# Attention in a hybrid decoder layer: values' products emitted three units behind the scores instead of two

## The chip, the cores and the metric

The kernel runs on one core of one Trainium2 chip. Its engines are TensorE (PE in the profile, its weight loads PEld), VectorE (DVE), ScalarE (ACT), GpSimd (POOL) and SyncE (SP), which issues most of the loads. The metric is device time of one execution in microseconds (us). The kernel before took 2129.9 us (median of 3 runs, 2129.59 to 2132.04).

## The reference

One inference step through two layers, for a prompt of 2048 tokens and for 8 sample sequences of 8 new tokens each with 1024 cached tokens. Layer 0 has a pooling mixer and differential attention side by side, layer 1 is gated linear attention. The change is in the prompt's attention of layer 0: 4 heads, each with two 64-wide query/key maps and a 128-wide value. For a block of 128 queries and all keys up to the diagonal:

```python
sc = jnp.einsum('bqhcd,bkhcd->bhcqk', qi, k)          # two maps c
sc = jnp.where((qpos[:, None] >= kpos[None, :])[None, None, None], sc, -jnp.inf)
p = jax.nn.softmax(sc, axis=-1)
a = p[:, :, 0] - lam_full * p[:, :, 1]
return jnp.einsum('bhqk,bkhe->bqhe', a, v)
```

The result is normalised per head (RMSNorm), multiplied by a gate and goes, together with the pooling mixer's output, through an output projection and a LayerNorm.

## The kernel before

**Units.** The prompt's attention is cut into 64 units (t, h): 128 queries of block t (0 to 15) of head h against 128 * (t + 1) keys. `units` (L1109) makes them in order: head 0 with all t; then head 1 with all t; then heads 2 and 3 in turn for each t. A unit has two parts.

`scores(t, h)` (L992): for each of the two maps c, the scores are matmuls into PSUM (L1016, L1017, the mask of the diagonal L1019), in pieces that hold two PSUM banks; there are two such places. DVE takes the negated row maximum (L1021 or L1024, joined by L1034), ACT writes the exponentials to SBUF and sums them (L1036). At the end DVE joins the two maps in the first one's buffer, `e0 + c2 * e1` (L1045), after the small steps L1039, L1043 and L1044.

`pv(t, h)` (L1051): for up to 4 blocks of 128 keys at a time, TensorE transposes the joined probabilities into one PSUM bank (L1068), ACT copies them out (`aT`, L1073), and TensorE multiplies them with the values into another bank (L1061). Then the result is copied (`oq`, L1088), and squares, RMS scale and gate follow on DVE and POOL (L1090 to L1099). For heads 0 and 1 the pair of blocks is stored (L1104); for heads 2 and 3 it stays in SBUF.

**Distance.** `self.pend` holds units whose scores are made and whose `pv` isn't. While the scores of a unit are emitted, the oldest of the list is emitted between them, piece by piece. `pend` is not emptied between the heads; `drain` (L1132) does it after the last unit.

**Buffers of the exponentials.** Four buffers (`ae0` to `ae3`, L919) and a fifth (`ae4`, L929) are in the list `self.e`. A unit takes two from its head (L1004) and writes map 0 to the first, map 1 to the second. The second comes back to the list's end after L1045 (L1047), the first when `pv` has emitted its last transposition (L1078). The two places come back in the order in which these are emitted. A new tenant's first write waits for the last reader of the old one.

**Values.** There is one place for the values of even heads and one for those of odd heads (L950), so head 3's first values (`vt`) are loaded when head 1's last products are done.

**What runs beside it.** `weave` (L869) emits other work between the units, in proportion to estimated costs: with head 0 the pooling mixer's part of the output projection (`out_pool`), with head 1 the whole attention of the samples (`Sample`, which loads the cached keys and values `sk` and `sv`), and with heads 2 and 3 the attention's part of the output projection and the LayerNorm (`out_attention`, L1196; its tiles are `otp`, `op`, `oyp`). A pair of tiles of the latter is emitted only when `A.done` (set at L1106) says that head 3's `pv` of a later block has been emitted (L1255). After that come layer 1's projections.

**Order.** The program text gives the order of emission. A planner then fixes each engine's own order before the program runs: in a simulated time of its own it takes, of the instructions that are ready, the one emitted first; the instructions of `scores` count as emitted 300 places earlier (`high_priority(300)`, L1011 and L1032). On the chip each engine goes through its fixed order and waits where an input or a buffer isn't ready.

Of the kernel before, what the change touches and what calls it, by code (L numbers as in the profile page):

```python
# [394 lines left out]
def layers(tc, d):  # L395
# [6 lines left out]
    with ExitStack() as left:  # L402
# [12 lines left out]
        for m, j in project_even(tc, d, P, P2, W, slot, psf):  # L415

            if (m, j) == (7, 3):

                keep = odd.enter_context(tc.tile_pool(name="keep", bufs=2, side="right", **rw))
                A = Attention(tc, d, right, psf, keep)  # L420
                A.load_k(0, 0)
                A.minus_lambda()
                A.load_q(0, 0)
            elif (m, j) == (5, 3):
                A.room_weights()
                units = A.units([0], [1])
            elif m == 3 and j % 2:
                next(units)
# [8 lines left out]
        A.load_v(0, 0)  # L437
        A.room_results()
        weave(units, fill, HEAD_COST, 17 * 8 * 640)
    with tc.tile_pool(name="as", bufs=2, **rw) as sp:  # L440
        weave(A.units([1], [2, 3]), Sample(tc, d, sp, A).gen(), HEAD_COST, 8 * 10300.0)
# [442 lines left out]
class Attention:  # L884
# [224 lines left out]
    def units(self, heads, after):  # L1109


        for t in range(16):
            for h in heads:
                if t % 4 == 2 and t < 14:
                    self.load_kv(h, t // 4 + 1)
                if t % 2 == 1 and t < 15:
                    self.load_q(h, t // 2 + 1)
                if t == 14 and h == heads[0]:
                    for n in after:
                        self.load_kv(n, 0)  # L1120
                        self.load_q(n, 0)
                old = self.pend.pop(0) if len(self.pend) == 2 else None
                for c in self.scores(t, h):
                    yield c
                    c = next(old, None) if old else None
                    if c is not None:
                        yield c
                if old:
                    yield from old
                self.pend.append(self.pv(t, h, *self.cur))  # L1130
# [1312 lines left out]
```

## Time and profile before

| | us |
|---|---|
| median of 3 runs | 2129.9 |
| the profiled execution's own time | 2135.73 |
| its span, first to last instruction | 2133.9 |
| TensorE busy | 2005.8 |
| VectorE busy | 1486.8 |
| ScalarE busy | 1005.2 |
| GpSimd busy | 878.9 |

The profile comes from one execution. A row of groups or of the timeline names the line of the kernel, the engine, the operation, what it writes and reads, its shape and how often it ran; then its busy time, the mean of one in ns, and the idle time of the engine just before it, with the instruction that ended that idle time (the releaser). The attention of head 0 runs from about 520 us, that of head 1 from about 710 us, that of heads 2 and 3 from about 880 to 1220 us.

### The profile page before, as it was taken

The page shows a single profiled execution, that of the slowest core. Times are in us where ns is not written, and L with a number is a line of the kernel's source. Part 1 is how long each engine was busy: PE and PEld are TensorE (multiplying, and loading weights), DVE is VectorE, ACT ScalarE, POOL GpSimd, SP SyncE. Part 2 cuts the span into 40 slices and gives each one's busy share as a digit, 9 for nine tenths or more (in the row PEclk, how much of TensorE's full clock was granted, in tenths as well). Part 3 has the DMA queues.
Part 4 walks back from the last instruction along what each step waited for, and adds up shares of the span by engine and source line. Part 5 has one row for each costly group of instructions (what it writes and reads, how often), then busy time and mean ns, then how long its engine had stood idle before and what let it go on. Part 6 is the DMA issues. An engine that isn't in the chain of part 4 may idle for free. (4 is left out here: it accounts for less than half of the span.)

```text
span 2133.9 us, 31445 instructions
## 1 busy us (share of the span) xinstructions
PE 2005.8 (94%) x10769; PEld 1641.6 (77%) x10769; DVE 1486.8 (70%) x2762; ACT 1005.2 (47%) x1910; POOL 878.9 (41%) x1163
## 2 busy tenths in 40 slices
PE   8999998999999999888898899999999997999998
PEld 7878786877788777677777678788888776888786
DVE  7697657565876676798767667756733647888884
ACT  4244433345633465665555443445425655555552
POOL 2345444323754542567643504222211223466554
PEclk9999999999899999999999999999999998999998
DMA  8877777547864588563322458765643557556532
GB/s 288 278 241 238 256 260 233 168 110 198 276 203 152 169 294 284 157 202 121 119 72 65 146 187 281 253 205 199 198 146 121 180 163 242 165 170 204 164 130 109
DMA packets 210973, 407.75 MB, mean 191 GB/s; under 512 B 29186, under 2 KB 106370, under 8 KB 210802
## 3 DMA queue, kind: packets, MB, share of 16 engines
q1 hardware_dynamic: 140354, 234.57, 36.1%
q0 software_dynamic: 49664, 156.39, 20.8%
q10 hardware_dynamic: 20784, 14.68, 2.2%
q8 instruction: 87, 1.43, 0.3%
q14 instruction: 84, 0.69, 0.1%
HBM read 277.99 MB, written 127.55 MB: 190 GB/s over the span
## 5 line engine op out<-in xcount | busy, mean ns | idle before, releaser
L1036 ACT ACTIVATE e<-sc,nm 128x896 f32<-128x896 f32 (+11 forms) x192 | 164.8, 864 | 125.5 <-DVE nm L1034 87.3
L1021 DVE TENSOR_REDUCE nm<-sc 128x1 f32<-128x768 f32 (+7 forms) x160 | 156.8, 991 | 27.9 <-PE sc L1017 16.3
L45 DVE TENSOR_TENSOR wk<-wr,wk 128x1024 fp32r<-128x1024 f32 x80 | 98.3, 1229 | 101.3 <-ACT wk L40 100.8
L45 DVE TENSOR_TENSOR wl<-wr,wh 128x1024 fp32r<-128x1024 f32 (+1 forms) x90 | 108.7, 1211 | 80.7 <-ACT wh L40 76.8
L1016 PE MATMUL sc<-kst,qh 128*128 128x512 f32 (+9 forms) x352 | 136.5, 391 | 29.3 <-ACT e L1036 28.2
L1061 PE MATMUL po<-vt,aT 128*128 128x128 f32 x1088 | 155.4, 282 | 2.2 <-ACT aT L1073 2.1
L40 ACT ACTIVATE wh<-wr 128x1024 fp32r<-128x1024 f32 (+1 forms) x85 | 88.0, 1038 | 138.7 <-PE f L52 62.4
L1061 PEld LDWEIGHTS po<-vt,aT 128*128 128x128 f32 x1088 | 140.4, 197 | 9.0 <-ACT aT L1073 2.4
L40 ACT ACTIVATE wk<-wr 128x1024 fp32r<-128x1024 f32 x77 | 81.4, 1058 | 134.1 <-PE f L53 96.2
L1073 ACT ACTIVATE aT<-tp 128x512 f32<-128x512 f32 (+3 forms) x160 | 85.4, 534 | 103.0 <-PE tp L1068 102.4
L1017 PE MATMUL sc<-kst,ql 128*128 128x512 f32 (+9 forms) x352 | 123.8, 354 | 0.0
L1016 PEld LDWEIGHTS sc<-kst,qh 128*128 128x128 f32 x352 | 69.3, 197 | 49.9 <-ACT e L1036 40.6
L1068 PE MATMUL tp<-ident,e 128*128 128x128 f32 x544 | 92.4, 285 | 13.1 <-ACT aT L1073 11.8
L1045 DVE SCALAR_TENSOR_TENSOR e<-e,c,e 128x128 f32<-128x128 f32 (+15 forms) x64 | 96.0, 1499 | 1.4
L1068 PEld LDWEIGHTS tp<-ident,e 128*128 128x128 f32 x544 | 64.5, 145 | 28.2 <-ACT aT L1073 16.7
L1017 PEld LDWEIGHTS sc<-kst,ql 128*128 128x128 f32 x352 | 69.7, 198 | 4.1 <-issue 0.2
L1039 DVE TENSOR_TENSOR s<-s 128x1 f32<-128x1 f32 x64 | 21.2, 331 | 70.2 <-ACT e L1036 69.9
L1092 POOL TENSOR_SCALAR s1q<-s 128x1 f32<-128x1 f32 x64 | 16.9, 266 | 104.4 <-DVE s L1039 79.5
L53 PE MATMUL op<-wh,ol 128*128 128x512 f32 x128 | 52.3, 408 | 5.1 <-DVE ol L1232 5.1
L51 PE MATMUL op<-wh,oh 128*128 128x512 f32 x128 | 53.1, 415 | 1.2 <-ACT oh L1231 1.2
L51 PE MATMUL gz<-wh,gmh 128*128 128x512 f32 x128 | 51.5, 406 | 1.8 <-ACT gmh L40 1.8
L53 PE MATMUL gz<-wh,gml 128*128 128x512 f32 x128 | 51.1, 402 | 1.9 <-DVE gml L45 1.9
(882 smaller groups left out, 6658.2 us busy)
## 6 DMA issues: line engine op xcount, KB each, us to landing
wr<-in_w_q SPq DMA_DIRECT2D x75, 512.0 KB, 4.9
wr<-pt SPq DMA_DIRECT2D x40, 512.0 KB, 7.3
wr<-rt SPq DMA_DIRECT2D x40, 512.0 KB, 4.2
sk<-in_cachek SPq DMA_DIRECT2D x64, 256.0 KB, 3.7
sv<-in_cachev SPq DMA_DIRECT2D x64, 256.0 KB, 4.8
pt<-pn POOLq DMA_DIRECT2D x32, 256.0 KB, 7.2
qr<-q SPq DMA_DIRECT2D x64, 128.0 KB, 3.9
kr<-k SPq DMA_DIRECT2D x32, 256.0 KB, 4.4
```

The lines of the kernel that those rows point to most:

```text
L40: h = nc.scalar.activation(hi, raw, AF.Copy)
L45: return h, (lo_eng or nc.vector).tensor_tensor(out=lo, in0=raw, in1=hi, op=ALU.subtract)
L51: nc.tensor.matmul(ps, lh(k), rh(k), start=(first and k == 0), stop=False, **kw)
L53: nc.tensor.matmul(ps, ll(k), rh(k), start=False, stop=(last and k == n - 1), **kw)
L1016: nc.tensor.matmul(o, qh[:, c, qs], kst[:, ks], start=True, stop=False)
L1017: nc.tensor.matmul(o, ql[:, c, qs], kst[:, ks], start=False, stop=k < npc - 1)
L1021: nc.vector.tensor_reduce(out=nm[:, c, i:i + 1], in_=p[:, :, :w], op=ALU.max, axis=AX.XY, negate=True)
L1036: nc.scalar.activation(o, p, AF.Exp, bias=nm[:, m, 0:1], accum_out=s[:, m, i if npc > 1 else 0:][:, :1])
L1045: nc.vector.scalar_tensor_tensor(out=es[0][:, :nk], in0=es[1][:, :nk], scalar=c2, in1=es[0][:, :nk], op0=ALU.mult, op1=ALU.add)
L1061: nc.tensor.matmul(po, s[:, 128 * j:128 * j + 128], vt[:, k0 + j, :], start=(k0 + j == 0), stop=(k0 + j == n - 1))
L1068: nc.tensor.transpose(p[:, 128 * j:128 * j + 128], a[:, 128 * (k0 + j):128 * (k0 + j) + 128], self.ident)
L1073: nc.scalar.activation(s[:, :128 * g], p[:, :128 * g], AF.Copy)
```

## The change

One number in `units`: the oldest waiting unit is taken for emission when three units wait, no longer when two do.

```diff
@@ -1119,7 +1119,7 @@
                     for n in after:
                         self.load_kv(n, 0)
                         self.load_q(n, 0)
-                old = self.pend.pop(0) if len(self.pend) == 2 else None
+                old = self.pend.pop(0) if len(self.pend) == 3 else None
                 for c in self.scores(t, h):
                     yield c
                     c = next(old, None) if old else None
```

The number of buffers, the loads and the work between the units are as they were.

## The prediction

> **What bounds the kernel now.** I read the page's first two parts, then busy time by stretches of 20 us, then the groups and waits, and last the order of single instructions.
>
> ```profile
> span 2133.9 us, 31445 instructions
> PE 2005.8 (94%) x10769; PEld 1641.6 (77%) x10769; DVE 1486.8 (70%) x2762; ACT 1005.2 (47%) x1910; POOL 878.9 (41%) x1163
> ```
>
> TensorE is the bound: its idle time is 2133.9 - 2005.8 = 128.1 us in all. The change touches only the prompt's attention. By stretches (us, length, then busy time and instructions of PE, PEld, DVE, ACT, POOL, then granted clock, DMA share, GB/s):
>
> ```profile
> 620.00:640.00 20.00, 20.00 (x110) 17.21 (x110) 13.81 (x25) 6.99 (x16) 9.84 (x13) 1.00 0.55 177
> 820.00:840.00 20.00, 20.00 (x197) 14.45 (x198) 15.39 (x34) 10.97 (x26) 6.20 (x8) 0.91 0.94 310
> 880.00:900.00 20.00, 14.85 (x113) 13.15 (x106) 16.25 (x26) 12.39 (x31) 19.23 (x19) 0.91 0.48 130
> 900.00:920.00 20.00, 14.47 (x77) 10.99 (x75) 19.73 (x54) 12.83 (x37) 9.55 (x14) 0.83 0.74 244
> 1140.00:1160.00 20.00, 16.37 (x100) 13.73 (x99) 14.81 (x27) 11.71 (x24) 9.24 (x10) 0.91 0.30 97
> ```
>
> With head 0 (first row) and head 1 (second) PE is full; with heads 2 and 3, from about 880 us, it idles 5.15, 5.53 and 3.63 us in the other three. What ends the idle time there, 880 to 1220 us, by groups (busy, mean ns | idle before, releasers):
>
> ```profile
> L1036 ACT ACTIVATE e<-sc,nm 128x1024 f32<-128x1024 f32 (+11 forms) x98 | 84.8, 871 | 59.1 <-DVE nm L1034 36.4 <-DVE nm L1021 8.4 <-DVE e L1045 6.0
> L1016 PE MATMUL sc<-kst,qh 128*128 128x384 f32 (+9 forms) x176 | 69.6, 398 | 18.3 <-ACT e L1036 18.1
> L1068 PE MATMUL tp<-ident,e 128*128 128x128 f32 x299 | 50.5, 285 | 9.3 <-ACT aT L1073 8.0 <-DVE lnso L1291 1.2
> ```
>
> The loop: scores fill PSUM, DVE takes their maximum, ACT's exponential empties PSUM, only then come the next scores (18.1 us of PE waiting). The transpositions that the change delays wait 8.0 us for the copy out of their PSUM bank and 1.2 us for a LayerNorm step; their input, written by L1045, is not among the releasers. **A longer distance between scores and values' products would remove a wait that costs next to nothing.**
>
> **The change part by part.** No instruction is added or removed; their order and two sets of waits change.
>
> *Work moves to later stages.* With three units waiting, the unit (t=13, head 0) is left to head 1's stage, and (13, 1) to the stage of heads 2 and 3. Head 1's stage gives what it gets, so the stages before 880 us lose 14 blocks in all. The price of a block:
>
> ```profile
> L1061 PE MATMUL po<-vt,aT 128*128 128x128 f32 x1088 | 155.4, 282 | 2.2 <-ACT aT L1073 2.1
> L1068 PE MATMUL tp<-ident,e 128*128 128x128 f32 x544 | 92.4, 285 | 13.1 <-ACT aT L1073 11.8
> ```
>
> A transposition takes 92.4/544 = 0.170 us of PE, a product instruction 155.4/1088 = 0.143, and each block has two of the latter: 0.456 us, so 14 blocks are 6.4 us. Taken out where PE is full, they bring the first scores of heads 2 and 3 forward; put back at 880 to 900 us, they find 5.15 us free. Ends: nothing, if head 1's stage ends by its cache loads (DMA share 0.94 at 820 us), and -6.4. I take half of the free room, **-2.6 us**.
>
> *The spare buffer goes.* Five buffers hold exponentials. A unit takes two from the head of `self.e`; one comes back when L1045 has joined the two maps, the other at the last transposition of that unit. With two units waiting, a starting unit finds three free. With three, it finds exactly two: that of the L1045 of the unit just before, and that of the transpositions of the unit four back. With heads 2 and 3, from (2,2) to (5,3) and from (8,3) to (13,3), it is the second exponential that must follow the L1045 of the unit before; in the other units it is the first. In large units there is room. Unit (10,2)'s L1045 and the second exponential of (10,3):
>
> ```profile
> 1042.87 1.69 DVE L1045 SCALAR_TENSOR_TENSOR e<-e,c,e 128x1408 f32<-128x1408 f32 x1
> 1051.70 0.85 ACT L1036 ACTIVATE e<-sc,nm 128x704 f32<-128x704 f32 x1 [0.50 <-PE tp L1068]
> ```
>
> That is 1051.70 - 1044.56 = 7.1 us to spare. In other places today's order is what the change forbids. L1045 of (3,2), (3,3), (4,3), (7,2) and (14,2), then ACT: second exponentials of (3,3), (4,2), (5,2), both of (7,3), the first of (14,3):
>
> ```profile
> 919.33 0.74 DVE L1045 SCALAR_TENSOR_TENSOR e<-e,c,e 128x512 f32<-128x512 f32 x1
> 922.87 1.00 DVE L1045 SCALAR_TENSOR_TENSOR e<-e,c,e 128x512 f32<-128x512 f32 x1
> 931.48 0.87 DVE L1045 SCALAR_TENSOR_TENSOR e<-e,c,e 128x640 f32<-128x640 f32 x1
> 963.47 1.28 DVE L1045 SCALAR_TENSOR_TENSOR e<-e,c,e 128x1024 f32<-128x1024 f32 x1
> 1160.75 2.21 DVE L1045 SCALAR_TENSOR_TENSOR e<-e,c,e 128x1920 f32<-128x1920 f32 x1
> ```
>
> ```profile
> 915.62 0.69 ACT L1036 ACTIVATE e<-sc,nm 128x512 f32<-128x512 f32 x1 [0.24 <-PE tp L1068]
> 922.65 0.79 ACT L1036 ACTIVATE e<-sc,nm 128x640 f32<-128x640 f32 x1
> 930.86 0.90 ACT L1036 ACTIVATE e<-sc,nm 128x768 f32<-128x768 f32 x1
> 960.38 1.16 ACT L1036 ACTIVATE e<-sc,nm 128x1024 f32<-128x1024 f32 x1
> 966.58 1.12 ACT L1036 ACTIVATE e<-sc,nm 128x1024 f32<-128x1024 f32 x1 [2.59 <-DVE nm L1021]
> 1160.93 1.06 ACT L1036 ACTIVATE e<-sc,nm 128x960 f32<-128x960 f32 x1 [0.90 <-DVE nm L1034]
> ```
>
> An exponential would have to start later by 920.07 - 915.62 = 4.45 us, 923.87 - 922.65 = 1.22, 932.35 - 930.86 = 1.49 and 1162.96 - 1160.93 = 2.03. In (7,3) the first is put off by 4.37 to 964.75, but with its 1.16 it still ends at 965.91, before the second (966.58) that waits for its maximum anyway: nothing. Behind a waiting exponential on ACT's queue stand the copies `aT` (L1073), which PE's products await, and PSUM stays full for the next scores. What of it reaches PE? Today 59.1 us of waiting ahead of exponentials go with 18.1 us of PE waiting for them: 0.306. At that rate the first three give (4.45 + 1.22 + 1.49) x 0.306 = 2.2 us; the last, in the chain of the largest units, I count in full: 2.0. **Together +4.2 us**; ends: nothing, where PE has other work, and 9.2 in full.
>
> A wait also goes: an exponential no longer waits for transpositions only three units back. From 880 to 1220 us (total, times, longest):
>
> ```profile
> ACT e L1036 <- PE tp L1068: 1.3, 4, 0.5
> ```
>
> At the same rate this gives **-0.4 us**; ends: 0 and -1.3.
>
> *What else the moved step issues.* Each moved unit takes along its copies on ACT, its L1090 and RMS steps on DVE and POOL, and for heads 0 and 1 a store on POOL's queue, read again only by the output projection (L1216) some stretches later. Head 3's values share a buffer with head 1's, so their load waits on SP's queue for head 1's last unit:
>
> ```profile
> 902.43 0.39 SPq L951 DMA_DIRECT2D vt<-v  x1
> 1226.83 0.48 PE L1227 MATMUL otp<-ident,oq 128*128 128x128 f32 x1 [6.10 <-POOL oq L1099]
> ```
>
> Head 1's last unit and head 3's first both come one unit later, so the distance stays: nothing, at most the 0.39 of an issue for what is queued behind. The output projection's tiles are released by `self.done`, one unit later as well; and after the last scores one more unit is queued ahead of the final 6.10 us wait. Ends: nothing, and 15 blocks, 15 x 0.456 = 6.8 us. I take nothing, because the planner already lets this work run as soon as its input is there: (13,2)'s L1045, then its first transpositions, emitted two units later:
>
> ```profile
> 1127.50 2.08 DVE L1045 SCALAR_TENSOR_TENSOR e<-e,c,e 128x1792 f32<-128x1792 f32 x1
> 1129.64 0.66 PE L1068 MATMUL tp<-ident,e 128*128 128x128 f32 x4
> ```
>
> 0.06 us lie between (1129.58 to 1129.64).
>
> **The sum:** -2.6 + 4.2 - 0.4 = +1.2 us. The profiled execution took 2135.73 us (span 2133.9 and 1.8 around it), so 2136.9 on its terms; it is 5.8 us above the median of 2129.9, and on that median I forecast **2131.1 us**.
>
> **The rivals.**
>
> A, *slower: the waits pass through.* If PE has nothing ready when an exponential waits, all four count in full, 9.2 us, and if nothing is won at 880 us the time is 2139.1. It decides where L1045 ends later than PE's last ready product. For it: 5.53 us of PE idle at 900 to 920 us with DVE busy 19.73 of 20. Against: 0.306.
>
> B, *the clock falls in the new waits.* Scores of (14,2) and (14,3) after waits of 1.35 and 2.31 us:
>
> ```profile
> 1157.30 0.38 PE L1017 MATMUL sc<-kst,ql 128*128 128x480 f32 x1
> 1157.51 0.38 PE L1016 MATMUL sc<-kst,qh 128*128 128x480 f32 x1
> 1162.13 0.77 PE L1016 MATMUL sc<-kst,qh 128*128 128x480 f32 x1 [2.31 <-ACT e L1036]
> 1162.70 0.60 PE L1017 MATMUL sc<-kst,ql 128*128 128x480 f32 x1
> 1163.10 0.60 PE L1016 MATMUL sc<-kst,qh 128*128 128x480 f32 x1
> ```
>
> They start 0.21 us apart, then 0.40. Eight of them lose 1.5 us; four waits, 6.1, on top of A: 2145.2. [...]
>
> C, *faster: the moved work is a full gain.* All 6.4 us and the 1.3 us of waits are won and the new waits fall where PE has work: 2122.2. For it: 5.15 us free at 880 us. Against: DMA at 0.94 just before.
>
> D, *the end grows.* One more unit after the last scores, 6.8 us, on the sum: 2137.9. Against: the 0.06 us above.
>
> E, *the change does little of what it says*, since the planner's order follows readiness: 2129.9.
>
> **How the numbers follow.** Forecast 0.30, A 0.19, B 0.07, C 0.28, D 0.11, E 0.05. 0.2% is 4.3 us, about what a measurement can tell from no change. Within it: E, most of the forecast (0.26) and a little of C (0.03), 0.34. Faster: the rest of C (0.25) and 0.02 of the forecast, 0.27. Slower: A, B, D and 0.02 of the forecast, 0.39. The planner reorders everything around the change, so C and D may overshoot; the range 2121 to 2146 leaves out about 0.05 below and 0.07 above. The forecast alone would be 2126 to 2136.
>
> **What would show it.** Right: L1045 as releaser of exponentials above 6.0 us after 880 us, that of transpositions below 1.3, PE busier at 880 to 900 than 14.85, its wait for exponentials near 18.1 + 4.2. Wrong: that wait above 27 us (A), more slow-clock stretches (B), PE still busy with products more than 6 us after the last L1045's own transpositions should end (D). If scores run ahead less because the buffers bind in the large units too, against the 7.1 us of room, all of this is too small.

## The result and the profile after

The changed kernel took **2150.1 us** (median of 4 runs, 2142.26 to 2156.37) against 2129.7 for the kernel before: a ratio of 1.009, interval 1.0069 to 1.0111, some 20 us slower. The forecast was 2131.1 with a range to 2146. The profiled execution took 2156.37 us. Single runs scatter: in one session the kernel before ran from 2124.96 to 2138.95 us (14 runs).

The first lines of the page of the changed kernel, then two of its stretches of 20 us (columns as in the prediction):

```profile
span 2154.6 us, 31441 instructions
PE 2013.4 (93%) x10769; PEld 1651.1 (77%) x10769; DVE 1480.4 (69%) x2762; ACT 1006.6 (47%) x1910; POOL 870.2 (40%) x1163
```

```profile
880.00:900.00 20.00, 12.70 (x81) 10.58 (x80) 17.31 (x29) 12.94 (x28) 18.09 (x16) 0.79 0.30 77
900.00:920.00 20.00, 12.32 (x72) 10.10 (x70) 15.45 (x35) 10.96 (x32) 9.54 (x13) 0.84 0.77 237
```

TensorE's idle time rose from 128.1 to 2154.6 - 2013.4 = 141.2 us, and its busy time by 7.6 us for the same 10769 instructions: they ran at a lower granted clock (0.965 in the mean, 0.975 before). At 880 to 900 us it was busy 12.70 us, where the forecast wanted more than the 14.85 of before. Waits of TensorE (the first row 880 to 1240 us, the second, the last wait of the stage, 880 to 1260), then of ACT, 880 to 1240 us:

```profile
PE sc L1016 <- ACT e L1036: 27.0, 14, 5.1
PE otp L1227 <- POOL oq L1099: 6.1, 1, 6.1
```

```profile
ACT e L1036 <- DVE nm L1034: 31.5, 19, 6.7
ACT e L1036 <- DVE rmoa L2320: 6.9, 2, 4.3
ACT e L1036 <- DVE e L1045: 4.6, 2, 3.7
```

The wait for exponentials grew from 18.1 to 27.0 us (25.5 in a second trace), where the forecast had 22.3; the last wait of the stage, 6.1 us, is what it was. L1045 as releaser of exponentials, which was to rise above 6.0, stands at 4.6 (7.6 in the second trace); the view puts some of these waits down to other steps, as shown below. To see where the time went, I matched each TensorE instruction with the same one in the trace of before and took how much later it starts. Between fixed points of the old trace (us, old trace's time; median of the instructions within 10 us of each point) the change gains or loses:

| three units back | heads 0, 1 (700 to 871) | change-over (871 to 925) | rest of heads 2, 3 (925 to 1255) | after (1255 to 2100) |
|---|---|---|---|---|
| the changed kernel | -5.0 | +14.5 | +6.0 | +0.7 |
| the same, second trace | -5.6 | +15.0 | +8.1 | -1.9 |

The first row's remaining 4.6 us stand before 700 us, nearly all of them (5.3 at 500) ahead of the attention; the second trace has -1.9 there, so that part varies from run to run. The change-over from head 1 to heads 2 and 3 is where most is lost. The two stretches, of before and of after, between the same instructions:

```profile
871.00:925.00 54.00, 41.95 (x323) 34.54 (x323) 45.59 (x105) 34.94 (x89) 37.40 (x41) 0.91 0.61 195
925.00:1255.00 330.00, 293.18 (x1759) 246.82 (x1758) 246.40 (x501) 172.59 (x360) 165.08 (x170) 0.96 0.36 111
```

```profile
870.60:939.10 68.50, 50.26 (x341) 40.34 (x340) 54.27 (x119) 39.32 (x95) 40.90 (x47) 0.80 0.62 185
939.10:1275.10 336.00, 295.83 (x1753) 251.13 (x1752) 240.28 (x495) 172.27 (x359) 156.01 (x163) 0.93 0.32 103
```

Of the 14.5 us at the change-over, 50.26 - 41.95 = 8.3 are busy time and 6.2 are idle. The busy time is moved work (18 more instructions, some 3 us at 0.143 to 0.170 each, an estimate) and a clock of 0.80 instead of 0.91. Of the idle time, TensorE's waits for exponentials rose by 2.0 (8.6 to 10.6); its transpositions waited 1.9 for a join, and a load added 1.4. What happens there, in order (start, length, engine; `kst` is the key of a coming block, split on POOL):

```profile
892.78 2.35 DVE L1045 SCALAR_TENSOR_TENSOR e<-e,c,e 128x2048 f32<-128x2048 f32 x1
895.39 8.44 DVE L2250 SCALAR_TENSOR_TENSOR ssq<-so,rmos,ssg 128x128 f32<-128x128 f32 x8
895.80 2.54 POOL L969 TENSOR_TENSOR kst<-kr,kst 64x512 fp32r<-64x512 f32 x2
899.09 2.51 POOL L969 TENSOR_TENSOR kst<-kr,kst 64x512 fp32r<-64x512 f32 x2
904.65 0.35 DVE L1045 SCALAR_TENSOR_TENSOR e<-e,c,e 128x128 f32<-128x128 f32 x1
905.09 0.37 ACT L1036 ACTIVATE e<-sc,nm 128x128 f32<-128x128 f32 x1 [3.70 <-DVE e L1045]
```

The first exponential of (0,3) at 905.09 waits for the L1045 of (0,2), which stands in DVE's queue behind L2250, the last step of the sampled rows, itself stretched to 8.44 us (3.42 before). In the kernel before only the second exponential of (0,3) needed that join, and L2250 came behind it.

### The profile page after: what moved, and what is told of

It is laid out like the page before. It is cut to its first block, busy times and chain, and to the rows that moved or that the text cites. A ratio compares the mean times of both kernels' runs of the same rounds, so it can differ in the third digit from the quotient of the medians.

```text
span 2154.6 us, 31441 instructions
## 1 busy us (share of the span) xinstructions
PE 2013.4 (93%) x10769; PEld 1651.1 (77%) x10769; DVE 1480.4 (69%) x2762; ACT 1006.6 (47%) x1910; POOL 870.2 (40%) x1163
## 5 line engine op out<-in xcount | busy, mean ns | idle before, releaser
L1036 ACT ACTIVATE e<-sc,nm 128x640 f32<-128x640 f32 (+11 forms) x192 | 164.8, 863 | 129.7 <-DVE nm L1034 83.2
L1068 PE MATMUL tp<-ident,e 128*128 128x128 f32 x544 | 95.0, 289 | 15.6 <-ACT aT L1073 10.9
L1045 DVE SCALAR_TENSOR_TENSOR e<-e,c,e 128x128 f32<-128x128 f32 (+15 forms) x64 | 94.4, 1474 | 1.2
L1068 PEld LDWEIGHTS tp<-ident,e 128*128 128x128 f32 x544 | 66.1, 148 | 30.2 <-ACT aT L1073 15.1
L1039 DVE TENSOR_TENSOR s<-s 128x1 f32<-128x1 f32 x64 | 22.9, 358 | 69.8 <-ACT e L1036 69.5
L45 POOL TENSOR_TENSOR ql<-qr,qh 128x512 fp32r<-128x512 f32 x31 | 42.9, 1383 | 44.3 <-ACT qh L40 43.2
L52 PE MATMUL op<-wl,oh 128*128 128x512 f32 x128 | 52.1, 407 | 0.0
```

The lines of the kernel that those rows point to most:

```text
L45: return h, (lo_eng or nc.vector).tensor_tensor(out=lo, in0=raw, in1=hi, op=ALU.subtract)
L1036: nc.scalar.activation(o, p, AF.Exp, bias=nm[:, m, 0:1], accum_out=s[:, m, i if npc > 1 else 0:][:, :1])
L1045: nc.vector.scalar_tensor_tensor(out=es[0][:, :nk], in0=es[1][:, :nk], scalar=c2, in1=es[0][:, :nk], op0=ALU.mult, op1=ALU.add)
L1068: nc.tensor.transpose(p[:, 128 * j:128 * j + 128], a[:, 128 * (k0 + j):128 * (k0 + j) + 128], self.ident)
```

## The experiments

Three theories stood at first: BUFFERS (only two are free, so exponentials wait for joins), START (the change-over) and CHANCE (any other order by the planner meets other collisions). A fourth, HELD, came from the trace. Medians are compared with the kernel before of the same session.

**The changed kernel again** (no edit).

> The changed kernel once more, for the spread of its times and a second trace. If its loss is its own, the median lies at 2145 to 2155 us again and the second trace gains some 6 us by 870 us and loses some 20 us between 880 and 915 us, as the first one does. If the loss is an accident of single runs, the times reach down to 2130 and the second trace loses its time in other places.

2150.2 us, ratio 1.0088 [1.0056, 1.012], and the loss in the same places (second row of the table): it is the kernel's own.

**The distance by stage.** `lag` replaces the constant in L1122, 2 or 3 by the first head of the stage:

```diff
+        lag = {0: 2, 1: 2, 2: 3}[heads[0]]      # second kernel: {0: 3, 1: 3, 2: 2}
+        while len(self.pend) > lag: yield from self.pend.pop(0)
-                old = self.pend.pop(0) if len(self.pend) == 2 else None
+                old = self.pend.pop(0) if len(self.pend) == lag else None
```

> Two units back with heads 0 and 1, three only with heads 2 and 3. Theory BUFFERS (with three units waiting only two exponential buffers are free, and exponentials wait for the joining L1045 of the unit before): the whole loss sits with heads 2 and 3 and the gain of some 6 us with heads 0 and 1 is absent, so 2150 to 2158 us. Theory START (the loss comes from the change-over at 880 us, where one more unit of head 1 and the last step of the sampled rows, L2250, stand ahead of the first joins of heads 0 to 3): the change-over is as in the kernel before, so 2130 to 2140 us. Theory CHANCE (the planner's order differs anywhere and any edit moves the time): no prediction better than 2120 to 2155 us.

> Three units back with heads 0 and 1, two with heads 2 and 3; the one unit too many is emitted ahead of the first scores of heads 2 and 3. Theory BUFFERS: what is lost with heads 2 and 3 is gone, the gain with heads 0 and 1 stays, so 2122 to 2128 us. Theory START: the change-over still has head 1's extra unit, ahead of the scores now, so 2140 to 2150 us. Theory CHANCE: 2120 to 2155 us.

Three units back for heads 2 and 3 alone: 2147.9, 1.0083 [1.0055, 1.0112], between START's and BUFFERS's ranges. For heads 0 and 1 alone: 2152.7, 1.0089 [1.0061, 1.0118], just above START's figure and far from BUFFERS's 2122 to 2128. Each half costs as much as the whole; they don't add. This fits CHANCE, whose range of 2120 to 2155, however, left little out.

**Buffers.** Packing: up to t = 7 both maps of a unit lie in one buffer, so a unit takes one place. Then two units back with one buffer fewer.

```diff
-        places = [self.e.pop(0) for _ in range(2)]
+        places = [self.e.pop(0) for _ in range(1 if t < 8 else 2)]
+        es = es if t >= 8 else [es[0][:, :NP // 2], es[0][:, NP // 2:]]
-                self.e.append(places[1])
+                self.e.extend(places[1:])
```

```diff
-        self.e.insert(0, self.pool("ae4", 1, side="right"))
```

> Three units back, but up to t = 7 the two maps of a unit share one exponential buffer (each takes at most half of it), so that two of the five stay free beside three waiting units and no exponential of those units needs the L1045 of the unit before. From t = 8 on nothing is changed. Theory BUFFERS: the wait of exponentials for L1045 is gone from 880 to some 985 us, the loss there (some 20 us at its peak, 10 kept) is gone too: 2130 to 2141 us. Theory START: L2250 stands ahead of the first joins as before and the transpositions behind them still come late: 2145 to 2155 us. Theory CHANCE: 2120 to 2155 us.

> Two units back, with the two maps of a unit up to t = 7 in one exponential buffer: the control for the run of the same packing three units back (2138 us). Theory BUFFERS: two units back no exponential waits long for a buffer, so the packing brings nothing, 2126 to 2137 us. If the packing itself gains, by some other way, it lies at 2112 to 2124 us, as far below the kernel before as the packed kernel three units back lies below the changed one.

> Two units back, but four exponential buffers in place of five: only two are free beside two waiting units, the same waits of an exponential for the L1045 of the unit before as in the changed kernel, without its later products. Theory BUFFERS: all of the loss, and without the gain of heads 0 and 1: 2148 to 2158 us. Theory HELD alone: the waits cost 4 us at most: 2128 to 2138 us. Theory CHANCE: 2120 to 2155 us, whatever the waits.

Packed, three units back: 2138.4, 1.0035 [1.0019, 1.0052]; packed, two units back: 2141.0, 1.0044 [1.0027, 1.0061]. So the packing costs some 9 us by itself, against BUFFERS's 2126 to 2137, but with it the distance costs nothing (-2.6). Four buffers: 2161.4, 1.0124 [1.0098, 1.0151], above even BUFFERS's range, with no product emitted later. In its trace (880 to 1240 us; its lines from the deleted one on count one less, so L1035 is L1036 and L1067 is L1068) the exponentials wait for buffers:

```profile
ACT e L1035 <- PE tp L1067: 14.8, 4, 7.2
ACT e L1035 <- DVE e L1044: 6.3, 3, 3.3
```

Scarce buffers are dear. But the packed kernel hit its forecast for another reason than the one given. TensorE's wait for exponentials fell, while most of the loss at the change-over stayed:

```profile
PE sc L1016 <- ACT e L1036: 13.2, 13, 1.7
```

```profile
857.20:921.60 64.40, 48.06 (x382) 40.14 (x381) 53.61 (x120) 42.11 (x104) 40.70 (x47) 0.92 0.63 192
```

Its change-over still takes 64.4 us where the kernel before takes 54.0: of the 10.4, 6.1 are busy time at a clock of 0.92, so moved work (382 instructions, not 323), and 4.3 are idle. It is the rest that is better (+3.0, against +15.1 for the packed kernel two units back).

**The change-over.** Turning the free list by one place, so that (0,2) takes buffers long free; taking L2250 off DVE; both; and three units back for head 1 alone.

```diff
+        while len(self.pend) > lag: yield from self.pend.pop(0); self.e.append(self.e.pop(0))
```

```diff
         for n in range(8):
-            nc.vector.scalar_tensor_tensor(out=sq[:, n, :], in0=self.o[:, n, :], scalar=sc[:, n:n + 1], in1=sg[:, n, :], ...)
+            nc.scalar.activation(sq[:, n, :], self.o[:, n, :], AF.Copy, scale=sc[:, n:n + 1])
+        nc.gpsimd.tensor_tensor(out=sq, in0=sq, in1=sg, op=ALU.mult)
```

> As the kernel with three units back only for heads 0 and 1, which lost 12 us between 871 and 925 us; its list of free exponential buffers is turned by one place at the change-over, so that unit (0, 2) starts with buffers given back by transpositions long done, and not with the one that the L1045 of (15, 1) gives back last. Nothing else is changed. Theory BUFFERS AT THE CHANGE-OVER (the four short units behind the longest one each wait for a join): the 12 us fall to 0 to 3, 2138 to 2144 us. Theory EXTRA UNIT (the loss is the extra unit of head 1 and its steps): no change, 2148 to 2158 us.

> The changed kernel with the last step of the sampled rows (L2250, 8.4 us of DVE at the change-over, held beside POOL's L969) taken from DVE: eight scalings on ACT, some 2.2 us, and one product on POOL, some 1.9 us. Theory L2250 (it stands ahead of the joins L1045 of the first units, and the exponential of (0, 3) waits 3.7 us for one of them): 5 to 9 us less than the changed kernel, 2141 to 2146 us. Theory BUFFERS without it: the exponential waits for another join instead, 2147 to 2153 us.

> Three units back for heads 0 and 1 only, with both edits of the change-over together: the free list turned by one place, and L2250 taken from DVE to ACT and POOL. Theory TWO CAUSES IN ONE PLACE (each alone let the other wait stand): the 10 us between 871 and 925 us fall to the moved work, 4 to 6, and the time to 2138 to 2146 us. Theory EXTRA UNIT (its products and their copies take the place of the first scores, whatever waits stand there): 10 us stay, 2147 to 2156 us.

> Three units back for head 1 alone; one extra unit is emitted ahead of the first scores of heads 2 and 3. Theory EXTRA UNIT at the change-over: 10 to 15 us lost between 871 and 925 us, some 5 gained before, 2140 to 2152 us. If the loss is made by head 0 and its hand-over to head 1, which is as in the kernel before here, it stays at 2126 to 2137 us.

The turned list: 2151.5, 1.0097 [1.008, 1.0114], no change. By the order of its instructions (0,2) got its buffers at once, and then the first exponential of (1,2) waited behind L2250 for its maximum:

```profile
892.88 8.46 DVE L2250 SCALAR_TENSOR_TENSOR ssq<-so,rmos,ssg 128x128 f32<-128x128 f32 x8
901.98 0.47 ACT L1036 ACTIVATE e<-sc,nm 128x256 f32<-128x256 f32 x1 [3.66 <-DVE nm L1024]
```

L2250 off DVE: 2154.3, 1.0104 [1.0087, 1.012], no gain either; now (0,3) waits for the join that the free list gives it:

```profile
899.13 0.37 ACT L1036 ACTIVATE e<-sc,nm 128x128 f32<-128x128 f32 x1 [3.34 <-DVE e L1045]
```

Each fix lays bare the other wait, at nearly the same length. Both at once: 2143.9, 1.0066 [1.0044, 1.0089], within TWO CAUSES by its time, but the change-over still lost 8.5 us, not 4 to 6, so that theory is not shown. Head 1 alone: 2144.9, 1.008 [1.0051, 1.0108], as EXTRA UNIT said, yet with +0.4 at the change-over and +9.6 in the rest, so for no reason of that theory. With five buffers, this loss stands only in traces with three units back in both stages ahead of it. The kernel with head 1 alone also has one more unit ahead of the first scores, and by its order of emission (0,2) and (0,3) get their buffers from the same steps as with three units back for heads 0 and 1, yet it loses 0.4 there. Why, stays open.

**Steps held on DVE.** In some of the changed kernel's largest waits a DVE step on 128x1 elements lasts until a POOL step ends, and the maximum behind it comes late. In the order of its instructions, the join of (11,3) and the maximum of (12,2):

```profile
1107.35 2.34 POOL L1304 TENSOR_TENSOR oz<-oz,lnb 128x1024 f32<-128x1024 f32 x1
1107.35 2.35 DVE L1044 SCALAR_TENSOR_TENSOR c<-s,nlam,c 128x1 f32<-128x1 f32 x1
1109.62 0.15 DVE L1034 TENSOR_TENSOR nm<-nm 128x1 f32<-128x1 f32 x1
1110.96 0.71 PE L1016 MATMUL sc<-kst,qh 128*128 128x416 f32 x1 [5.14 <-ACT e L1036]
```

L1044 takes 0.22 us in the median of its 34. Theory HELD: the output projection's LayerNorm on POOL holds DVE, and the change moved the hits onto L1034. The test gives that step to DVE for every tile:

```diff
-        ln.finish(d["y0"][t0:t0 + n, :], i in (14, 15))
+        ln.finish(d["y0"][t0:t0 + n, :], True)
```

> Two units back as in the kernel before; the last step of the output projection's LayerNorm (L1302 to L1304, 1.2 + 2.4 + 2.3 us on POOL for a tile) goes to DVE as four steps of 128x512 for every tile, as tiles 14 and 15 do already. Theory HELD (DVE's small steps of 0.15 to 0.22 us last up to 2.4 us when POOL runs L1303 or L1304, some 40 us in all with heads 2 and 3 in either kernel; the changed kernel loses because more of it falls on L1034, the maximum that the exponential waits for): the held time falls to a third, PE's wait for exponentials falls below 15 us and the time to 2115 to 2126 us. Theory BUFFERS says nothing of this kernel: 2126 to 2136 us, as DVE gains as much work as it loses in held time. Theory CHANCE: 2120 to 2150 us.

> Three units back as in the changed kernel, with the same move of the LayerNorm's last step to DVE. Theory HELD: the loss of the change goes with the held steps, so within 6 us of the kernel two units back with the same move, 2115 to 2132 us. Theory BUFFERS: the waits for L1045 stay, so 15 to 20 us above that kernel. Theory CHANCE: anywhere between 10 below and 25 above it.

> Three units back with the packing up to t = 7 and with the LayerNorm's last step on DVE. If buffers up to t = 7 and steps held behind POOL's LayerNorm are the whole loss, it comes within 6 us of the kernel two units back with the LayerNorm on DVE (2108 us): 2102 to 2115 us. If three units back cost something else, in the large units above all, it stays 15 us and more above that: 2123 to 2140 us.

> Two units back, packing up to t = 7 and the LayerNorm's last step on DVE: the control for the same kernel three units back (2122 us). Theory BUFFERS (the distance itself costs nothing where buffers are free): 2116 to 2128 us. Theory DISTANCE (three units back costs by itself, beside the buffers): near the kernel two units back with the LayerNorm on DVE alone, 2102 to 2113 us.

Two units back: **2108.2 us, 0.9883 [0.9857, 0.9909]**, better than both kernels and below HELD's range. Three units back: 2139.5, 1.0029 [1.0014, 1.0044]: 31 us above it where HELD said within 6 and BUFFERS 15 to 20. So held steps are a cost of both kernels, not the cause of this change's loss. What went: the busy time of groups of small DVE steps, in the kernel before (870 to 1250 us) and in the two-unit kernel with this edit (870 to 1230 us); last, the latter's rest of heads 2 and 3:

```profile
L1044 DVE SCALAR_TENSOR_TENSOR c<-s,nlam,c 128x1 f32<-128x1 f32 x33 | 18.0, 544 | 0.6
L1039 DVE TENSOR_TENSOR s<-s 128x1 f32<-128x1 f32 x34 | 14.2, 419 | 32.1 <-ACT e L1036 31.9
L1034 DVE TENSOR_TENSOR nm<-nm 128x1 f32<-128x1 f32 x34 | 9.5, 280 | 0.2
```

```profile
L1044 DVE SCALAR_TENSOR_TENSOR c<-s,nlam,c 128x1 f32<-128x1 f32 x33 | 13.0, 393 | 0.5
L1039 DVE TENSOR_TENSOR s<-s 128x1 f32<-128x1 f32 x34 | 6.8, 199 | 22.5 <-ACT e L1036 22.1
L1034 DVE TENSOR_TENSOR nm<-nm 128x1 f32<-128x1 f32 x34 | 5.8, 171 | 0.3
```

```profile
921.90:1229.00 307.10, 284.59 (x1752) 242.13 (x1751) 242.38 (x561) 173.49 (x360) 68.61 (x110) 0.98 0.39 120
```

POOL's busy time falls from 165.08 to 68.61 us and DVE's does not rise (246.40 to 242.38), though it takes on four steps a tile: time in which it was held has gone (41.6 to 9.4 us in the small steps alone, see the last section). The stretch takes 22.9 us less. With the packing as well, three units back: 2122.3, 0.9956 [0.9939, 0.9973], between the two ranges; two units back: 2118.3, 0.9939 [0.9916, 0.9963], as BUFFERS said. Once more the distance costs little (+4.1) where buffers are free.

**The order alone.** Neutral edits: the weight of the weaving, once for the last stage only, then for all three, and that also three units back.

```diff
-        weave(last(), fill, 2 * HEAD_COST, 17 * (8 * 640 + 1320.0), drain=False)
+        weave(last(), fill, 1.8 * HEAD_COST, 17 * (8 * 640 + 1320.0), drain=False)
```

```diff
-HEAD_COST = 76000.0
+HEAD_COST = 78000.0      # another kernel: 74000.0
```

> The kernel before with one number changed: the output projection is woven into heads 2 and 3 at 2 / 1.8 of its rate (1.8 HEAD_COST in place of 2), so that some of its steps are emitted a little earlier; heads 0 and 1 and the distance stay. Theory CHANCE (the order before is a good one of many, any other order in this stage meets other collisions): 8 to 25 us slower, with L1034 held more often than 3 times. Theories BUFFERS and HELD by the distance alone: 2125 to 2137 us.

> The kernel before with one number changed: the estimated cost of a head by which the other work is woven in (HEAD_COST) is 78000 in place of 76000. The order changes in all three stages, the distance and the buffers do not. Theory CHANCE: 8 to 25 us away from the kernel before, slower more likely than faster. If the order alone is worth little: 2126 to 2138 us.

> The kernel before with HEAD_COST at 74000, a neutral edit of the other sign. Theory CHANCE (the order before is a good one among many): 6 to 20 us slower again, 2138 to 2152 us. If the loss at 78000 was a single accident: 2126 to 2136 us.

> The changed kernel with HEAD_COST at 78000 in place of 76000, the neutral edit that cost 15 us two units back (2147 us). Theory BUFFERS: the distance costs its 15 to 30 us under this order too, 2162 to 2177 us. Theory CHANCE: the loss of the change is that of an unlucky order, and a new order draws again: 2135 to 2158 us.

Last stage only: 2132.7, 0.9994 [0.9975, 1.0014]. 78000: 2147.3, 1.0071 [1.0046, 1.0096], 15 us for nothing but another order. 74000: 2138.4, 1.0027 [1.0009, 1.0045]. 78000 and three units back: 2159.9, 1.0135 [1.011, 1.016], 12.6 above its two-unit kernel, just short of BUFFERS's 15 and above CHANCE's range. CHANCE alone had forecast a cost for the three edits two units back: it missed the first (8 to 25 slower), had the second (the same) and just had the third (2138 to 2152). The rest of heads 2 and 3 in the kernel with 78000, two units back, takes 342.2 us, longer than the changed kernel's 336.0:

```profile
922.60:1264.80 342.20, 296.90 (x1755) 250.30 (x1754) 246.42 (x499) 174.12 (x360) 164.68 (x169) 0.95 0.34 108
```

**All pairs of the distance** (medians, us):

| | two units back | three units back | difference |
|---|---|---|---|
| as it is | 2131.2 | 2150.2 | +19 |
| HEAD_COST 78000 | 2147.3 | 2159.9 | +13 |
| LayerNorm on DVE | 2108.2 | 2139.5 | +31 |
| packed up to t = 7 | 2141.0 | 2138.4 | -3 |
| packed, LayerNorm on DVE | 2118.3 | 2122.3 | +4 |

**And all traces by stretch** (us against the trace of before; the kernel with three units back in heads 2 and 3 only has the same order as before up to 880 us and shows -2.5 there, so some 3 us are noise):

| | heads 0, 1 | change-over | rest of heads 2, 3 |
|---|---|---|---|
| three units back in heads 0 and 1 (10 traces: the changed kernel twice, 78000, LayerNorm, packed, packed and LayerNorm, L2250 off DVE, heads 0 and 1 only, turned, turned with L2250 off) | -2.6 to -8.0 | +8.5 to +16.1 | +3.0 to +15.2; LayerNorm on DVE -8.4 and -17.1 |
| two units back (last stage's weight, 74000, 78000, packed, packed and LayerNorm, LayerNorm) | -3.3 to +1.3 | -2.7 to +4.8 | +0.5 to +15.1; LayerNorm on DVE -3.6 and -22.9 |
| three units back in head 1 only; in heads 2 and 3 only | +3.7; -2.5 | +0.4; +2.2 | +9.6; +8.9 |

With five buffers the change-over tells the first two rows apart in every trace. The rest does not: an order two units back can lose as much there. The kernel with four buffers, two units back, loses 9.6 us at the change-over and 17.7 in the rest, like one three units back. A sixth buffer, the plainest test of BUFFERS, was not tried.

## Why the prediction was wrong

- **Work moves to later stages (-2.6).** Half right, then wrong in sign. The gain ahead of 871 us came nearly in full (-5.0 of -6.4). But the moved work did not find the 5.15 us that TensorE had free at 880 us: at the change-over idle time grew by 6.2 us instead, and busy time by 8.3. The idle time of before consisted mostly of waits for exponentials (8.6 of 12.1 us at 871 to 925), and more products did not fill it. Net of the two stretches: +9.5 instead of -2.6. This is the first step that failed. Which part of the +14.5 comes with the moved work, and which with the waits, the falling clock and the new order, is not shown.
- **The spare buffer goes (+4.2, at most 9.2).** The mechanism is there and the term is mis-sized. Where only two buffers are free, the distance costs 13 to 31 us in three orders; where the short units need one each, -3 to +4; and one buffer fewer two units back costs 27 us. TensorE's wait for exponentials rose by 8.9 instead of 4.2. My sum counted four exponentials that today's order puts ahead of a join. Of these, two were seen waiting at that place: the second of (3,3) by 0.87 us instead of 4.45, and the first of (14,3) by 2.25, as forecast (2.03):

```profile
1178.06 2.21 DVE L1045 SCALAR_TENSOR_TENSOR e<-e,c,e 128x1920 f32<-128x1920 f32 x1
1180.38 1.06 ACT L1036 ACTIVATE e<-sc,nm 128x960 f32<-128x960 f32 x1 [2.65 <-DVE rmoa L2320]
```

  It starts 0.11 us after the join ends, 2.25 after its own maximum (1177.98 + 0.15); the view names the DVE step that ended next. Exponentials that start right behind a join and later than their maximum and the ACT step ahead of them add up to 10.9 us in 5 places (14.1 in 6 in the second trace), against 5.2 in 3 before. So the increase, 5.7 to 8.9 us, was no larger than the 9.2 that the forecast had in full, but it fell in other places: 3.70 are that of (0,3) at the change-over, and the second of (2,3) waited 0.60, which my list left out though in the trace of before it began at 907.17, ahead of the end of (2,2)'s join at 908.79. The next largest, 3.46, is that of (6,2) for the join of (5,3):

```profile
957.52 3.25 DVE L1045 SCALAR_TENSOR_TENSOR e<-e,c,e 128x768 f32<-128x768 f32 x1
957.55 2.40 POOL L1304 TENSOR_TENSOR oz<-oz,lnb 128x1024 f32<-128x1024 f32 x1
960.86 1.01 ACT L1036 ACTIVATE e<-sc,nm 128x896 f32<-128x896 f32 x1 [3.46 <-DVE c L1043]
```

  This join lasted 3.25 us beside L1304, 1.02 in the trace of before, so here a scarce buffer and a held step act together; TensorE had products of the projection meanwhile and did not idle. What made 20 us of such waits is not shown. Three things came with them: the planner lays the whole order out anew, joins stand behind other steps on DVE, and TensorE's granted clock falls (0.965 in the mean, from 0.975).
- **Transpositions no longer waited for (-0.4).** Right: they are no releaser of exponentials any more.
- **What else moves (0).** Right for the end: the last wait is 6.1 us as before, so rival D is out.
- **Rival A, the waits pass through.** Its sign, a wait above 27 us, is met at its limit at most (27.0, 25.5 in the second trace), and its 2139.1 is 11 us short.
- **Rival B, the clock.** Nearest in time (2145.2), and in part what happened: the mean granted clock fell from 0.975 to 0.965. It was an addition to full waits of four exponentials; the fall was from 0.91 to 0.80 at the change-over and from 0.96 to 0.93 in the rest.
- **The range.** The planner's order was taken as something that follows readiness, worth at most a little on either side. A neutral edit moves the time by 15 us. No sum of local waits made on the old order can be trusted to 10 us here; the range should have reached some 15 us to either side of each case.

What remains open: how much of the 19 us is the distance and how much the order that came with it. The pairs say that scarce buffers make the distance dear on average, +21 against +1, but with a scatter of orders of up to 15 us five pairs don't give a size, and in the packed kernels the gain does not stand at the change-over, where the theory had put it.

## What to carry to other kernels

Before you lengthen a software pipeline, count the buffers that stay free at the moment a stage starts, above all where a long unit is followed by short ones: idle time of the busiest engine at such a place can be a chain of dependences that moved work does not fill. Where a planner orders the whole program, run one or two neutral edits first: they tell how large a difference must be before it says anything of your change. The profile's largest gain here lay elsewhere, in small steps of one engine that last as long as another engine's large ones (L1044: 0.22 us in the median, 2.35 beside L1304).

## What the runs showed of the hardware

In these traces small DVE steps are held beside POOL's. Between 870 and 1250 us 32 DVE steps on 1 or 2 elements a partition, 0.15 to 0.22 us otherwise, lasted over 0.4 us longer in the kernel before, 41.6 us in all (40.2 in 31 in the changed one), and 9.4 us in 10 with the LayerNorm off POOL. Each of the 32 ended 0.006 to 0.024 us after a POOL step did; L1044 above ended 0.01 us after L1304. Of the 32, 30 read two operands from SBUF (L1034, L1039, L1044, L2319, L2320, L2325); the other two are of L2322, which reads one of 2 elements (2.32 us beside L1303 in one of them). L1043, which reads one of 1 element, never lasted over 0.17. Why a POOL step holds them is not shown.

In the changed kernel the granted clock fell behind each of TensorE's two longest waits for exponentials, of 3.47 us (ended 1070.11) and 5.14 us (1110.96): from 0.96 at 1060 to 1070 us to 0.53, and from 1.00 at 1100 to 1110 to 0.66.

```profile
1070.00:1080.00 10.00, 9.20 (x30) 7.62 (x31) 5.33 (x13) 4.45 (x11) 0.50 (x2) 0.53 0.18 66
1110.00:1120.00 10.00, 9.04 (x45) 8.46 (x46) 4.60 (x10) 5.40 (x11) 2.88 (x6) 0.66 0.18 66
```

At 0.53 the first of these stretches loses some 0.47 x 9.20 = 4.3 us of work beside the wait itself, an estimate that takes the pace as proportional to the clock: in the kernel before, the scores of 128x480 started 0.21 us apart at 1.00 (1157 to 1160 us) and 0.40 apart at 0.50 (1162.1 to 1164). Four waits of 1.75 to 2.32 us between 890.9 and 906.0 in the changed kernel went with low clocks as well, 0.79 at 880 to 900 us and 0.84 at 900 to 920. How long a wait has to be for that is not shown.
